# Latent attention: high and low parts of the rotated queries stacked on the array's two halves of rows, two score passes for three

## Chip, cores and metric

One core of a Trainium2 chip runs the whole program. The metric is the device time of one execution in microseconds (us), as the median of several runs. The profile comes from one execution of its own.

## What is computed

The reference is a stack of four transformer-like blocks (windowed attention, latent attention, a recurrent mixer, grouped-query attention). The change touches the second one only. Its core, cut to what matters:

```python
def mla_attend(qn, qp, kn, kp, v):
    scale = (MLA_NOPE + MLA_ROPE) ** -0.5          # 128 and 64
    s = (jnp.einsum('bqhd,bkhd->bhqk', qn, kn)
         + jnp.einsum('bqhr,bkr->bhqk', qp, kp)).astype(jnp.float32) * scale
    p = jax.nn.softmax(s, axis=-1).astype(v.dtype)
    return jnp.einsum('bhqk,bkhd->bqhd', p, v)
```

There are 16 heads, 256 queries and 512 keys (256 context and 256 latent tokens). A score is the sum of a plain part of width 128, with keys of each head, and a rotated part (rope) of width 64, whose key `kp` is one for all heads.

## The kernel before

All products run in the type fp32r, and to keep float32 accuracy every operand is held as two tiles, a high part (the value cast to fp32r) and a low part (the value less its high part). `mm3` (line 349) makes a product of three matmuls, which this text calls passes: high x high, high x low, low x high (lines 352, 353, 354). The product of the two low parts is left out. `hilo` (433) makes the parts: ScalarE casts (436), VectorE subtracts (437).

`mla` (783) works on head groups of two heads (`HG`), eight groups. `project(g + 1)` makes the operands of the next group: it loads weights (`weights`, 327, on the SyncE queue), splits them into `whi` on ScalarE (323) and `wlo` on VectorE (324), multiplies, normalises (`head_norm`, 606) and transposes to feature-major layout (`to_feat`, 640). `project` and the gate's projection are a generator, and `work` (424) takes some steps of it between the attention steps of the current group (`STEPS`), so that TensorE has projections to do while the softmax of a head runs on VectorE and ScalarE. Beside this, `fill` (284) advances a second generator, `mod_steps` (243), which loads tiles of `mod_w` (1 MB each, line 240) into one buffer `mraw` in this stage and multiplies them (line 260).

`head_norm` for rotated queries: a copy of the bank (611), ScalarE's square (613), VectorE's sum (615), a scaling (453), the power -1/2 on GpSimd (456), then four VectorE steps (621, 624, 628, 629) for norm and rotation. Its tiles, `hr`, `sq` and `w`, come from one ring of four scratch tiles (`t512`, 146). The rotated queries of four heads are made at a time: every second head group, for two token tiles of 128 tokens each (lines 868 to 876). A normalised tile isn't transposed at once: it goes into the list `late`, and the oldest entry is transposed when more than `LATE` = 2 are in it. The rotated query tiles are `qph` and `qpl`, with 64 rows in use; the rotated keys are `kph` and `kpl` (`ev_kv`, 814), also with 64 rows, made once for each of four token tiles before the head loop.

The scores of a head and one token tile go into one PSUM bank: three passes over 128 rows of the array for the plain part, three over 64 rows for the rotated part (lines 925, 926). `probs` (552) takes the maximum, the exponential and the scaling; `attend` (575) transposes the probabilities (591) and multiplies with the values.

Which instruction runs when on an engine is decided by the framework's scheduler when the program is built; on the chip each engine keeps that order, and semaphores make it wait for the others. Work of different parts of the text is therefore interleaved on every engine.

Of the kernel before, what the change touches and what calls it, by code (L numbers as in the profile page):

```python
# [10 lines left out]
F32 = mybir.dt.float32  # L11
F32R = mybir.dt.float32r
AF = mybir.ActivationFunctionType
ALU = mybir.AluOpType
# [4 lines left out]
P = 128  # L19
D = 2048  # L20
KD = D // P
NT = 512
NC = 256
L = 64
HG = 2
# [91 lines left out]
class Net:  # L117
# [665 lines left out]
    def mla(self, kvb):  # L783
        nc, I, h = self.nc, self.I, self.h
        scale = 192 ** -0.5
        with self.tc.tile_pool(name="mla", bufs=1) as ph:
# [2 lines left out]
            tk = self.rope_tables(ph, I["pe_cos"], I["pe_sin"], "mk_pe", "mk_pes", 64, "mk")  # L789
            ckh = ph.tile([P, 2, NT], F32R, name="ckh")  # L790
            ckl = ph.tile([P, 2, NT], F32R, name="ckl")
            kph = ph.tile([64, 1, NT], F32R, name="kph")
            kpl = ph.tile([64, 1, NT], F32R, name="kpl")
            cqh = ph.tile([P, 4, NC], F32R, name="cqh")
            cql = ph.tile([P, 4, NC], F32R, name="cql")

            def low(ps, n, nb, dh, dl, s, gain):
                sq = self.t512("sq", cols=n)
                ss = self.small(1, "ss")
                nc.scalar.activation(sq, ps, AF.Square, accum_out=ss)  # L800
                rs = self.small(1, "rs")
                self.rpow(rs, ss, 1.0 / n, EPS)
                q = self.t512("cq", cols=n)
                nc.vector.tensor_scalar(q, ps, rs, None, ALU.mult)
                pb = self.bank("tr")
                for b in range(nb):
                    nc.tensor.transpose(pb[:, b * P : (b + 1) * P], q[:, b * P : (b + 1) * P], self.ident)
                for b in range(nb):
                    self.hilo(dh[:, b, s], dl[:, b, s], pb[:, b * P : (b + 1) * P], self.v(gain, b))
# [4 lines left out]
            def ev_kv(t, ps):  # L814
                s = slice(t * P, (t + 1) * P)
                rope = None if t < 2 else (tk[0][:, t - 2, :], tk[1][:, t - 2, :])
                kp = self.head_norm(ps[:, 256:320], 1, 64, gain=self.row("mk_pe"), rope=rope)
                self.to_feat(kp, 1, 64, kph[:, :, s], kpl[:, :, s])
                low(ps[:, 0:256], 256, 2, ckh, ckl, s, "kva_g")

            def ev_cq(t, ps):
# [2 lines left out]
            for t in range(4):  # L824
                ev_kv(t, kvb[t])
# [3 lines left out]
            qp = {}  # L829

            def two_toks(w, act, kc, toks):

                ws = list(self.weights(w, kc, HG * P))
                for t0 in toks:
                    bank = self.acc()
                    for t in (t0, t0 + 1):
                        s = slice(t * P, (t + 1) * P)
                        out = bank[:, (t - t0) * HG * P : (t - t0 + 1) * HG * P]
                        for k, wh, wl in ws:
                            self.mm3(out, act[0][:, k, s], act[1][:, k, s], wh, wl, k == 0, k == kc - 1)  # L840
                        yield None
                    yield t0, bank

            def project(g, t_):

                new = lambda n, shape: ph.tile(shape, F32R, tag=n, name=self.nm(n), bufs=2)
                kq = {n: new(n, [P, HG, NT]) for n in ("kh", "kl")}
                kq.update({n: new(n, [P, 4, HG * P]) for n in ("vh", "vl")})
                kq.update({n: new(n, [P, HG, NC]) for n in ("qh", "ql")})
                t_.update(kq)  # L850
                late = []

                def norms():

                    for got in two_toks(I["mla_kb"][g], (ckh, ckl), 2, (0, 2)):
                        yield
                        if got:
                            k = self.head_norm(got[1], 2 * HG, P)
                            s = slice(got[0] * P, (got[0] + 2) * P)
                            late.append((k, 2 * HG, P, *(pairs_of(kq[n], s) for n in ("kh", "kl"))))  # L860
                            yield "group"
                    for got in two_toks(I["mla_qb"][g], (cqh, cql), 4, (0,)):
                        yield
                        if got:
                            q = self.head_norm(got[1], 2 * HG, P)
                            late.append((q, 2 * HG, P, *(pairs_of(kq[n], slice(0, NC)) for n in ("qh", "ql")), self.qkg))
                            yield "group"
                    if g4 not in qp:
                        qp[g4] = [ph.tile([64, 4, NC], F32R, tag=n, name=self.nm(n), bufs=2) for n in ("qph", "qpl")]
                        banks = {}  # L870
                        yield from self.mm_tok_steps(banks, I["mla_qp"][g4], (cqh, cql), 4, 256, range(2))
                        for t in range(2):
                            s = slice(t * P, (t + 1) * P)
                            q = self.head_norm(banks[t][:, :256], 4, 64, rope=(tq[0][:, t, :], tq[1][:, t, :]))
                            late.append((q, 4, 64, qp[g4][0][:, :, s], qp[g4][1][:, :, s]))
                            yield "group"
                    for got in two_toks(I["mla_vb"][g], (ckh, ckl), 2, (0, 2)):
                        yield
                        if got:
                            v = got[1].rearrange("p (t d) -> p t d", t=2)  # L880
                            self.hilo(kq["vh"][:, got[0] : got[0] + 2, :], kq["vl"][:, got[0] : got[0] + 2, :], v)
                            yield "group"

                g4 = g * HG // 4
                for what in norms():
                    yield
                    if what and len(late) > LATE:
                        self.to_feat(*late.pop(0))
                        yield
                while late:  # L890
                    self.to_feat(*late.pop(0))
                    yield

            def pairs_of(t, s):
                return t[:, :, s].rearrange("p h (t q) -> p t h q", t=2)

            def jobs(g, nxt, banks):

                gate, owed = self.gate_job(I["mla_g"][g], NC, banks, HG), 0.0
                for _ in project(g + 1, nxt) if g + 1 < 16 // HG else ():  # L900
                    yield
                    owed += GRATE[g % 2]
                    while owed >= 1.0:
                        owed -= 1.0
                        if next(gate, "end") != "end":
                            yield
                yield from gate

            cur = {}
            for _ in project(0, cur):  # L910
                pass
            for g in range(16 // HG):
                oT = ph.tile([P, HG, NC], F32, tag="oT", name=self.nm("oT"), bufs=2)
                oT = [oT[:, hh, :] for hh in range(HG)]
                banks, nxt = [], {}
                self.beside(jobs(g, nxt, banks), STEPS[g % 2] if g < 7 else 16, (1 + 2 * MB + MT) * HG)
                kh, kl, vh, vl, qh, ql = (cur[n] for n in ("kh", "kl", "vh", "vl", "qh", "ql"))
                qph, qpl = qp[g * HG // 4]
                for hh in range(HG):
                    hd = HG * g + hh  # L920
                    prs = []
                    for t in range(2):
                        s = slice(t * P, (t + 1) * P)
                        sc = self.bank("sc")
                        self.mm3(sc, qh[:, hh, s], ql[:, hh, s], kh[:, hh, :], kl[:, hh, :], True, False)
                        self.mm3(sc, qph[:, hd % 4, s], qpl[:, hd % 4, s], kph[:, 0, :], kpl[:, 0, :], False, True)
                        prs.append(self.probs(sc, NT, scale, None, ph, hd))
                    self.work()
                    po = self.bank("pv")
                    self.attend(  # L930
                        prs, NT, lambda c: vh[:, c, hh * P : (hh + 1) * P], lambda c: vl[:, c, hh * P : (hh + 1) * P],
                        po[:, :NC], ph, bool(MB),
                    )
                    nc.scalar.copy(oT[hh], po[:, :NC])
                    if MT:
                        self.work()
                self.work(last=True)
                self.gate_out(oT, HG * g, banks, NC, self.oscr, ph)
                cur = nxt
# [1060 lines left out]
```

## Time and profile before

| | |
|---|---|
| median of 3 runs | 3359.38 us (3355.93 to 3361.99) |
| profiled execution | 3360.43 us, its span 3358.6 us |
| TensorE (PE) busy | 3206.8 us, 95% |
| VectorE (DVE) busy | 2050.3 us, 61% |
| ScalarE (ACT) busy | 1543.9 us, 46% |
| granted TensorE clock, mean | 0.984 of full speed |

The span is what the profiler recorded from the first to the last instruction; the execution's time has some 1.8 us more around it. A share of busy time is a mean over stages with different limits, so a change in one stage is judged from that stage's own window. Matmuls are pipelined: the next one starts before the one before it has ended, so the cost of a pass is the distance from its start to the next start. PE is the matmuls, PEld the loading of the stationary operand, which can run beside a matmul. A form such as 64\*128 is the part of the array in use, rows by columns.

### The profile page before, as it was taken

Reading aid. Unit: us, or ns where it says so; the run is one execution under the profiler, and the core shown is the slowest. Engines: PE = TensorE matmul, PEld = TensorE weight load, DVE = VectorE, ACT = ScalarE, POOL = GpSimd, SP = SyncE. Lnnn points to the kernel's source line nnn. Section 1 sums busy time; section 2 is a strip of 40 time slices with the busy share of each in tenths; the row PEclk is TensorE's granted clock in tenths of the full one; section 3 lists DMA queues with packets and bytes.
Section 4 is the critical chain, followed back from the end, with each engine's and each line's share of the span. In section 5 each row is a group of like instructions: output and inputs, shape, how many; then the busy total and the mean of one; then the engine's idle time right before and its main releaser. Section 6 shows DMA issues by size and latency. Waiting matters only on the chain.

```text
span 3358.6 us, 56061 instructions
## 1 busy us (share of the span) xinstructions
PE 3206.8 (95%) x21218; PEld 2374.5 (71%) x21218; DVE 2050.3 (61%) x4487; ACT 1543.9 (46%) x3461; POOL 195.4 (6%) x277
## 2 busy tenths in 40 slices
PE   5999999999999999999999999999999999899997
PEld 2567777767777777886666666566666668678887
DVE  2446455543476665557766777577677536857766
ACT  2424444442366565643444444343444423646654
POOL 0000000000001010000000000000000001200000
PEclk8999999989999999999999999999999999999999
DMA  7843434357654655765333333334334464534354
GB/s 302 307 163 127 145 138 145 131 191 288 224 164 147 212 197 204 278 228 173 119 117 117 117 114 106 105 96 150 115 107 135 173 237 139 182 126 138 136 175 155
DMA packets 270784, 556.27 MB, mean 166 GB/s; under 512 B 122928, under 2 KB 150704, under 8 KB 244912
## 3 DMA queue, kind: packets, MB, share of 16 engines
q1 hardware_dynamic: 270512, 552.68, 48.5%
q8 instruction: 167, 2.74, 0.3%
q14 instruction: 105, 0.86, 0.1%
HBM read 517.46 MB, written 35.13 MB: 165 GB/s over the span
## 4 chain that ended last, share of the span: by engine, by line
PE 80%; DVE 8%; DMA 4%; ACT 3%; issue 2%; POOL 2%; SPq 0%; POOLq 0%; DVEq 0%; ACTq 0%
PE a L352 19%; PE a L354 17%; PE a L353 17%; PE mv L260 6%; PE gram L1241 2%; DMA mraw<-mod_w 2%; POOL rs L456 2%; PE ptr L591 1%; PE sc L352 1%; DVE wlo L324 1%; PE chain L1376 1%; PE chain L1380 1%; PE inv L1341 1%; PE chain L1388 1%; ACT whi L323 1%
## 5 line engine op out<-in xcount | busy, mean ns | idle before, releaser
L324 DVE TENSOR_TENSOR wlo<-raw,whi 128x512 fp32r<-128x512 f32 (+2 forms) x1000 | 659.8, 667 | 592.1 <-ACT whi L323 556.2
L352 PE MATMUL a<-hhi,whi 128*128 128x512 f32 (+1 forms) x2752 | 976.8, 356 | 15.4 <-ACT whi L323 11.0
L323 ACT CAST whi<-raw 128x512 fp32r<-128x512 f32 (+2 forms) x1000 | 593.3, 599 | 826.4 <-PE a L353 471.6
L354 PE MATMUL a<-hhi,wlo 128*128 128x512 f32 (+1 forms) x2752 | 947.5, 348 | 5.9 <-DVE wlo L324 5.5
L353 PE MATMUL a<-hlo,whi 128*128 128x512 f32 (+1 forms) x2752 | 952.1, 346 | 0.1
L352 PEld LDWEIGHTS a<-hhi,whi 128*128 128x128 f32 x2752 | 522.9, 190 | 160.3 <-issue 52.8
L354 PEld LDWEIGHTS a<-hhi,wlo 128*128 128x128 f32 x2752 | 520.8, 190 | 70.6 <-DVE wlo L324 11.4
L353 PEld LDWEIGHTS a<-hlo,whi 128*128 128x128 f32 x2752 | 523.8, 190 | 55.1 <-issue 4.1
L352 PE MATMUL a<-whi,hhi 128*128 128x512 f32 (+1 forms) x672 | 261.9, 400 | 18.5 <-ACT sq L613 5.9
L260 PE MATMUL mv<-mraw,cs 128*32 128x512 f32 x1536 | 251.0, 634 | 19.5 <-DMA mraw<-mod_w 19.2
L353 PE MATMUL a<-wlo,hhi 128*128 128x512 f32 (+1 forms) x672 | 263.8, 393 | 0.3
L456 POOL TENSOR_TENSOR rs<-st,mhalf 128x4 f32<-128x4 f32 (+3 forms) x109 | 140.4, 1288 | 2102.2 <-DVE st L453 1952.0
L354 PE MATMUL a<-whi,hlo 128*128 128x512 f32 (+1 forms) x672 | 259.7, 389 | 0.1
L352 PEld LDWEIGHTS a<-whi,hhi 128*128 128x128 f32 x672 | 126.6, 190 | 76.3 <-issue 22.2
L353 PEld LDWEIGHTS a<-wlo,hhi 128*128 128x128 f32 x672 | 128.6, 191 | 30.1 <-DVE wlo L324 4.6
L354 PEld LDWEIGHTS a<-whi,hlo 128*128 128x128 f32 x672 | 128.4, 191 | 26.4 <-issue 1.1
L565 ACT ACTIVATE pr<-sc,nm 128x512 f32<-128x512 f32 (+1 forms) x128 | 81.1, 633 | 93.1 <-DVE nm L562 66.7
L1385 ACT ACTIVATE SD<-SV,DL 64x64 f32<-64x64 f32 x224 | 77.2, 345 | 80.4 <-DVE SV L1399 77.2
L1399 DVE SCALAR_TENSOR_TENSOR SV<-chain,DL,SD 64x64 f32<-64x64 f32 x224 | 63.3, 283 | 71.2 <-PE chain L1393 62.9
L556 DVE TENSOR_REDUCE mx<-sc 128x1 f32<-128x512 f32 (+1 forms) x128 | 79.0, 617 | 41.6 <-PE sc L354 24.7
L260 PEld LDWEIGHTS mv<-mraw,cs 128*32 128x32 f32 x1536 | 36.1, 110 | 93.0 <-issue 52.2
L572 ACT ACTIVATE pr<-pr,rc 128x512 f32<-128x512 f32 (+1 forms) x128 | 85.6, 669 | 22.0 <-DVE rc L571 21.9
(371 smaller groups left out, 4460.3 us busy)
## 6 DMA issues: line engine op xcount, KB each, us to landing
mraw<-mod_w SPq DMA_DIRECT2D x192, 1024.0 KB, 4.9
raw<-od_in SPq DMA_DIRECT2D x88, 512.0 KB, 3.3
raw<-swa_in SPq DMA_DIRECT2D x72, 512.0 KB, 3.3
raw<-ev_rkv SPq DMA_DIRECT2D x64, 384.0 KB, 3.5
raw<-ev_in SPq DMA_DIRECT2D x48, 512.0 KB, 3.7
raw<-swa_out SPq DMA_DIRECT2D x40, 512.0 KB, 5.6
raw<-ev_out SPq DMA_DIRECT2D x40, 512.0 KB, 3.4
raw<-mla_g SPq DMA_DIRECT2D x64, 256.0 KB, 3.0
```

Source lines behind the costliest of these rows:

```text
L260: nc.tensor.matmul(pb[32 * j : 32 * j + 32, :], cs[:, 32 * k + 30 - 2 * n : 32 * k + 62 - 2 * n], raw[:, j, :], start=(n == 0 and q == 0), ...
L323: nc.scalar.copy(whi, raw)
L324: nc.vector.tensor_tensor(wlo, raw, whi.bitcast(F32), op=ALU.subtract)
L352: mm(out, ah, bh, start=first, stop=False, skip_group_check=shared)
L353: mm(out, ah, bl, start=False, stop=False, skip_group_check=shared)
L354: mm(out, al, bh, start=False, stop=last, skip_group_check=shared)
L456: self.nc.gpsimd.tensor_tensor(dst, stv, mv, op=ALU.pow)
L556: nc.vector.reduce_max(mx, sc, axis=AX.X)
L565: nc.scalar.activation(pr[:, :n], sc, AF.Exp, scale=scale, bias=nm, accum_out=sm)
L572: nc.scalar.activation(pr[:, :n], pr[:, :n], AF.Copy, scale=rc)
L1241: mm(pb[:, (c - c4) * P : (c - c4 + 1) * P], lhs, AQ[r_, hh, c, :], start=True, stop=True)
L1385: nc.scalar.activation(SD[r_], SV[r_, hh, c, :], AF.Copy, scale=DL[r_, c : c + 1])
```

## The change

The rotated queries get one tile `qp` of 128 rows: rows 0 to 63 hold the high part, rows 64 to 127 the low part of the same 64 features. The rotated keys are stored twice, in both halves of `kph` (high parts) and of `kpl` (low parts). One pass with `kph` then gives high x high plus low x high, one with `kpl` high x low plus low x low: two passes over 128 rows in place of three over 64 rows. (The product of the low parts, left out before, is now included.)

To bring the same values into both halves, `twice` copies a normalised token-major tile on ScalarE so that each head's 64 columns stand there two times (128 columns); the transposes then give 128 rows. `stack` replaces `to_feat` for the queries: four transposes, a cast of all 128 rows, and on VectorE, for rows 64 to 127 alone, the subtraction of the just cast values in place. For the keys, `to_feat` is called with 128 rows instead of 64. Entries of `late` for the rotated queries have two members, by which `feat` tells them from the others.

```diff
--- before.py
+++ after.py
@@ -789,8 +789,29 @@
             tk = self.rope_tables(ph, I["pe_cos"], I["pe_sin"], "mk_pe", "mk_pes", 64, "mk")
             ckh = ph.tile([P, 2, NT], F32R, name="ckh")
             ckl = ph.tile([P, 2, NT], F32R, name="ckl")
-            kph = ph.tile([64, 1, NT], F32R, name="kph")
-            kpl = ph.tile([64, 1, NT], F32R, name="kpl")
+
+
+            kph = ph.tile([P, 1, NT], F32R, name="kph")
+            kpl = ph.tile([P, 1, NT], F32R, name="kpl")
+
+            def twice(q, nh):
+
+                t = self.t512("tw", cols=nh * P)
+                nc.scalar.copy(
+                    t.rearrange("p (h a d) -> p h a d", h=nh, a=2),
+                    q.rearrange("p (h d) -> p h d", h=nh).unsqueeze(2).broadcast_to([P, nh, 2, 64]),
+                )
+                return t
+
+            def stack(q, dst):
+
+                pb = self.bank("tr")
+                for n in range(4):
+                    nc.tensor.transpose(pb[:, n * P : (n + 1) * P], q[:, n * P : (n + 1) * P], self.ident)
+                pv = pb.rearrange("p (h t) -> p h t", h=4)
+                nc.scalar.copy(dst, pv)
+                lo = slice(64, P)
+                nc.vector.tensor_tensor(dst[lo], pv[lo], dst[lo].bitcast(F32), op=ALU.subtract)
             cqh = ph.tile([P, 4, NC], F32R, name="cqh")
             cql = ph.tile([P, 4, NC], F32R, name="cql")
 
@@ -815,7 +836,7 @@
                 s = slice(t * P, (t + 1) * P)
                 rope = None if t < 2 else (tk[0][:, t - 2, :], tk[1][:, t - 2, :])
                 kp = self.head_norm(ps[:, 256:320], 1, 64, gain=self.row("mk_pe"), rope=rope)
-                self.to_feat(kp, 1, 64, kph[:, :, s], kpl[:, :, s])
+                self.to_feat(twice(kp, 1), 1, P, kph[:, :, s], kpl[:, :, s])
                 low(ps[:, 0:256], 256, 2, ckh, ckl, s, "kva_g")
 
             def ev_cq(t, ps):
@@ -866,13 +887,13 @@
                             late.append((q, 2 * HG, P, *(pairs_of(kq[n], slice(0, NC)) for n in ("qh", "ql")), self.qkg))
                             yield "group"
                     if g4 not in qp:
-                        qp[g4] = [ph.tile([64, 4, NC], F32R, tag=n, name=self.nm(n), bufs=2) for n in ("qph", "qpl")]
+                        qp[g4] = ph.tile([P, 4, NC], F32R, tag="qp", name=self.nm("qp"), bufs=2)
                         banks = {}
                         yield from self.mm_tok_steps(banks, I["mla_qp"][g4], (cqh, cql), 4, 256, range(2))
                         for t in range(2):
                             s = slice(t * P, (t + 1) * P)
                             q = self.head_norm(banks[t][:, :256], 4, 64, rope=(tq[0][:, t, :], tq[1][:, t, :]))
-                            late.append((q, 4, 64, qp[g4][0][:, :, s], qp[g4][1][:, :, s]))
+                            late.append((twice(q, 4), qp[g4][:, :, s]))
                             yield "group"
                     for got in two_toks(I["mla_vb"][g], (ckh, ckl), 2, (0, 2)):
                         yield
@@ -882,13 +903,18 @@
                             yield "group"
 
                 g4 = g * HG // 4
+
+                def feat():
+                    args = late.pop(0)
+                    (stack if len(args) == 2 else self.to_feat)(*args)
+
                 for what in norms():
                     yield
                     if what and len(late) > LATE:
-                        self.to_feat(*late.pop(0))
+                        feat()
                         yield
                 while late:
-                    self.to_feat(*late.pop(0))
+                    feat()
                     yield
 
             def pairs_of(t, s):
@@ -915,7 +941,7 @@
                 banks, nxt = [], {}
                 self.beside(jobs(g, nxt, banks), STEPS[g % 2] if g < 7 else 16, (1 + 2 * MB + MT) * HG)
                 kh, kl, vh, vl, qh, ql = (cur[n] for n in ("kh", "kl", "vh", "vl", "qh", "ql"))
-                qph, qpl = qp[g * HG // 4]
+                qpe = qp[g * HG // 4]
                 for hh in range(HG):
                     hd = HG * g + hh
                     prs = []
@@ -923,7 +949,8 @@
                         s = slice(t * P, (t + 1) * P)
                         sc = self.bank("sc")
                         self.mm3(sc, qh[:, hh, s], ql[:, hh, s], kh[:, hh, :], kl[:, hh, :], True, False)
-                        self.mm3(sc, qph[:, hd % 4, s], qpl[:, hd % 4, s], kph[:, 0, :], kpl[:, 0, :], False, True)
+                        for n, kp in enumerate((kph, kpl)):
+                            nc.tensor.matmul(sc, qpe[:, hd % 4, s], kp[:, 0, :], start=False, stop=n == 1)
                         prs.append(self.probs(sc, NT, scale, None, ph, hd))
                     self.work()
                     po = self.bank("pv")
```

## Rows read from the trace of the kernel before

**Rows 1.** The page: busy us of each engine (share) xinstructions.
```profile
PE 3206.8 (95%) x21218; PEld 2374.5 (71%) x21218; DVE 2050.3 (61%) x4487; ACT 1543.9 (46%) x3461; POOL 195.4 (6%) x277
```

**Rows 2.** Windows, head loop: length; PE, PEld, DVE, ACT, POOL busy; clock, DMA.
```profile
1036.60:1343.40 306.80, 299.15 (x2123) 237.21 (x2120) 187.72 (x403) 182.64 (x396) 29.30 (x27) 0.99 0.57 198
```

**Rows 3.** Waits of PE's matmuls, the same stretch: total us, times, longest.
```profile
PE a L354 <- DVE wlo L324: 2.8, 3, 1.2
PE a L352 <- ACT whi L323: 2.1, 3, 1.1
PE a L353 <- DVE wlo L324: 1.2, 3, 0.4
```

**Rows 4.** Timeline of PE, two scores of one head: start us, us, instruction.
```profile
1203.19 0.28 PE L354 MATMUL a<-hhi,wlo 128*128 128x256 f32 x1
1203.31 0.39 PE L352 MATMUL sc<-kh,qh 128*128 128x512 f32 x1
1203.54 0.40 PE L353 MATMUL sc<-kl,qh 128*128 128x512 f32 x1
1203.77 0.40 PE L354 MATMUL sc<-kh,ql 128*128 128x512 f32 x1
1204.10 0.50 PE L352 MATMUL sc<-kph,qph 64*128 64x512 f32 x1
1204.44 0.39 PE L353 MATMUL sc<-kpl,qph 64*128 64x512 f32 x1
1204.67 0.38 PE L354 MATMUL sc<-kph,qpl 64*128 64x512 f32 x1
1204.99 0.50 PE L352 MATMUL sc<-kh,qh 128*128 128x512 f32 x1
...
1206.76 0.38 PE L353 MATMUL a<-wlo,ckh 128*128 128x256 f32 x1
1206.99 0.28 PE L354 MATMUL a<-whi,ckl 128*128 128x256 f32 x1
```

**Rows 5.** Tile kh, 32 first passes: idle before its instructions, us, times.
```profile
  issue: 5.0, 14
```

**Rows 6.** Tile kph: one of the three rotated passes; duration ns min/median/max.
```profile
L354 PE MATMUL sc<-kph,qpl x32: 383/393/393, 1038.9 to 1343.0; 64*128 64x512 f32 x32
```

**Rows 7.** Tile qph: its cast and the subtraction after it.
```profile
L436 ACT CAST qph<-tr x8: 579/581/583, 1031.1 to 1287.6; 64x512 fp32r<-64x512 f32 x8
L437 DVE TENSOR_TENSOR qpl<-tr,qph x8: 671/674/683, 1032.6 to 1288.3; 64x512 fp32r<-64x512 f32 x8
```

**Rows 8.** Tile tr, 960:1360 us: the cast of a full-height tile.
```profile
L436 ACT CAST kh<-tr x16: 563/584/591, 1020.6 to 1326.4; 128x512 fp32r<-128x512 f32 x16
```

**Rows 9.** Line L480: a copy with each value repeated 64 times, on ACT.
```profile
L480 ACT COPY rse<-rs x16: 602/608/618, 1532.8 to 2528.8; 128x512 f32<-128x512 f32 x16
```

**Rows 10.** Timeline, the first score of the head loop.
```profile
1037.08 0.58 ACT L436 CAST qph<-tr 64x512 fp32r<-64x512 f32 x1 [0.99 <-PE tr L644]
1037.70 0.68 DVE L437 TENSOR_TENSOR qpl<-tr,qph 64x512 fp32r<-64x512 f32 x1 [0.44 <-ACT qph L436]
1038.26 0.60 PE L352 MATMUL sc<-kph,qph 64*128 64x512 f32 x1
```

**Rows 11.** Timeline, normalisation of one rotated query tile: square to last rotation step.
```profile
1104.63 0.38 ACT L613 ACTIVATE sq<-a 128x256 f32<-128x256 f32 x1
1105.90 1.30 POOL L456 TENSOR_TENSOR rs<-st,mhalf 128x4 f32<-128x4 f32 x1 [11.31 <-DVE st L453]
...
1109.30 0.41 DVE L629 TENSOR_TENSOR hr<-hr,w 128x256 f32<-128x256 f32 x1
```

**Rows 12.** Waits of ACT, the head loop.
```profile
ACT hr L637 <- POOL rs L456: 30.3, 19, 3.7
```

**Rows 13.** Tile mraw, the head loop: 32 loads, their time to landing, waits.
```profile
L240 SPq DMA_DIRECT2D mraw<-mod_w x32: 327/328/984, 1053.9 to 1325.1; - x32
DMA to landing us min/median/max: 4.6/4.8/6.8
```

## The prediction

> **What bounds the kernel now.** I read the page first, then the stretch that the change touches, then the passes themselves. On the page TensorE is busy for 95% of the span, VectorE for 61%, ScalarE for 46% [rows 1]. Such a share mixes stages, so the windows view of the latent attention's head loop comes next, from its first score (1036.6 us) to its last (1343.4 us): 306.80 us long, PE busy for 299.15 of them, DVE for 187.72, ACT for 182.64, clock 0.99 [rows 2]. PE's idle time is 306.80 - 299.15 = 7.65 us, and the waits list gives its three largest causes, all for weights that ACT and DVE convert: 2.8 + 2.1 + 1.2 = 6.1 us [rows 3]. So PE sets the pace of this stretch, and a pass taken off PE should come off the time, unless what PE rarely waits for today comes late.
>
> What a pass costs is read from starts, not durations, because passes overlap. Back-to-back 128-row passes with 512 columns start 0.23 us apart (1203.31, 1203.54, 1203.77), those with 256 columns 0.12 apart (1203.19, 1203.31). Two 64-row passes with 512 columns also start 0.23 apart (1204.44, 1204.67): half the rows gain nothing. But each change of height costs extra: 1203.77 to 1204.10 is 0.33, 1204.10 to 1204.44 is 0.34, back to 128 rows 1204.67 to 1204.99 is 0.32, and after the second score a 256-column pass takes 1206.76 to 1206.99, 0.23 for 0.12 [rows 4]. So a change of height costs 0.10 before the first pass of the new height and 0.11 at it, 0.2 us in all. That it is the height and not the new accumulation is seen at tile kh: of 32 first passes of a score, 14 show an unexplained idle time ahead of them, 5.0 us in all, 0.36 each [rows 5]. The loop has 16 heads with two scores each, and the program text puts these two next to each other, so some 16 first passes follow a 64-row group and some 16 a 128-row pass; the one at 1203.31 is of the second sort and starts at the ordinary pitch.
>
> **Passes removed.** One head's two scores run from 1203.31 to 1206.76, and 0.11 of the pass after them is still theirs: 3.45 + 0.11 = 3.56 us for 12 passes. Afterwards they are ten 128-row passes: 10 x 0.23 = 2.30 us. That is 1.26 us for a head. A rotated pass occurs 32 times [rows 6], so there are 16 such pairs: 16 x 1.26 = 20.2 us off PE. Of these 32 x 0.23 = 7.4 us is the third pass, and 12.8 us is 64 changes of height at 0.2.
>
> A sentence of the Trainium skill speaks against counting this in full: "Perfetto Trace Analysis", section Identifying the Most-Contended Engine, says that matmul busy time is a poor measure of a loaded TensorE and that weight loading's busy share is a good one. Here that share is 237.21 of 306.80, 77% [rows 2]; read so, 77% of the saving, 15.6 us, would show. The starts leave no free slot between passes [rows 4], so the trace speaks for the whole; no term below hangs on this.
>
> **Transposes, cast, subtraction.** Their number stays. The query cast grows from 64 to 128 rows: 581 ns [rows 7] against 584 for a full-height cast [rows 8], 0. The subtraction keeps its 64 x 512 (674 ns [rows 7]), but writes rows 64 to 127: 0. DVE and POOL get no new instruction. No DMA is added or moved, so no queue's order changes by design. The query tiles shrink to one where there were two; nothing uses the space.
>
> **Copies added.** `twice` puts each value into both halves, on ACT. The nearest row is a copy that spreads values over 128x512: 608 ns [rows 9]. Eight query tiles cost 8 x 0.61 = 4.9 us, two of them ahead of the loop; the four key tiles are a quarter of the width, so between 0.15 and 0.61 each. In the loop ACT goes from 182.6 to 186.3 us of some 287, hidden as long as PE's converted weights are ready. Bounds for what PE feels: below, 0; above, a doubling of PE's waits on ACT and DVE, 6.1 us [rows 3]. I take 2, nearer to 0: ACT and DVE are idle a third of the loop, but the loop is 7% shorter. The copy's target is from the ring of four scratch tiles; it is asked for when the tile w is done with, which the copy waits for anyway: 0.
>
> **Start of the loop.** The first score waits for its query tile. Before, the first rotated pass (1038.26) needs only the cast (1037.08 + 0.58), and the low part comes from DVE by 1038.38 [rows 10]. Afterwards the first rotated pass needs the low part as well, and the copy of 0.61 stands ahead of the transposes. Between 0 (the three other passes of the score cover it) and 0.61 + 0.68 + the keys' 4 x 0.61 = 3.7 us; I take 1.5, a copy and a subtraction with a little cover. Later query tiles are made one head group ahead.
>
> **Sum.** Profiled execution 3360.43 (span 3358.6 and 1.8 around it) - 20.2 + 2 + 1.5 = 3343.7. The median of the runs, 3359.38, is 1.05 below the profiled one: 3342.7, forecast 3343. Its own range: with no cost at all 3359.4 - 20.2 = 3339.2, with both upper bounds 3359.4 - 20.2 + 6.1 + 3.7 = 3349.0; runs of before differ by 3 either way, and a changed loop shifts the whole order that the scheduler makes: 3336 to 3352.
>
> **Rivals.** *The switch stays.* If the 0.2 us belongs to the change from one operand group to another and not to the height, only the pass goes: 7.4 - 3.5 = 3.9 us, 3355. For it: the rotated passes are never seen at full height. Against: the pass at 1203.31 changes operands at the ordinary pitch [rows 4]. Chance 0.07.
>
> *Given back.* The mod_w tiles go through one buffer in this stage: 32 loads in 306.8 us, one each 9.6 us, landing takes 4.8 (at most 6.8) [rows 13]. A loop shorter by 20 us leaves 9.0 for each, still over 6.8 and the eight passes that free the buffer; only where two steps lie close would PE wait longer. With converted weights late as well, at most the whole 20.2 is given back: 3354 to 3359. Chance 0.08.
>
> *ACT's queue stands behind the copy (slower).* The copy can't run before the last rotation step. One query tile's square starts at 1104.63, POOL's power takes 1105.90 to 1107.20, the last step ends at 1109.71: 1109.71 - 1105.01 = 4.7 us from the square's end [rows 11]. If ACT's order has the copy right behind the square, the weight casts queued behind it wait that long, and PE waits for them and for DVE's subtractions from them. Six copies in the loop x 4.7 = 28 us against 20.2 saved and 1.5 lost at the start: 3359.4 - 20.2 + 1.5 + 28 = 3369. It decides from (20.2 - 1.5) / 6 = 3.1 us of PE stall for each copy. For it: ACT already stands 30.3 us in the loop for POOL's power, in 19 waits of up to 3.7 [rows 12]. Against: all of those leave PE 2.1 us of waits for ACT [rows 3], and between the square and the last step much other work runs on both engines, so the order isn't that of the program text. In a sentence of its own: the Trainium skill, "TensorE: Matmul & The Clock Gate", section Architectural detail, calls ACT's queue a strict FIFO, by which such a copy would block what is behind it; the 30.3 us agree. Chance 0.07.
>
> That the change doesn't do what it says is hardly possible: the passes are written out one by one.
>
> **Chances.** Forecast 0.78, the others 0.07, 0.08, 0.07. A measurement tells 0.2% (6.7 us) from no change: faster 0.78, same 0.15, slower 0.07. The range takes the forecast's, the first rival and half of the second: 3336 to 3357.
>
> **What would show it.** In the trace after: score passes at 0.23 us from first to last, no 0.36 us of weight-load idle before them, `twice` at some 0.6 us, PE busy in the head loop some 20 us less. Wrong would be: 0.33 us between the nope and the rotated passes (the switch stays); PE waits on whi and wlo of over 12 us, or mraw waits of several us (given back); ACT idle of 4 us before each copy with PE idle beside it (slower).

## The result, and the profile after

| | before | after |
|---|---|---|
| median of the runs | 3360.31 us | 3344.61 us |
| ratio after/before, 95% interval | | 0.9949 (0.9932 to 0.9966) |
| profiled execution, its span | 3358.6 us | 3342.8 us |
| head loop, first to last start of a score pass | 306.3 us | 286.8 us |
| from the end of the key/value projection to the first score | 65.5 us | 69.1 us |
| from the last score pass to the end | 2015.6 us | 2015.7 us |

The changed kernel was measured a second time, beside other kernels (label c_after): median 3342.22 us, ratio 0.9949 (0.9935 to 0.9963). So the change makes the kernel 0.5% faster, 17 us with an interval of some 6 either way, and the profiled executions differ by 15.8 us. One of the changed kernel's five executions in the table took 16649.97 us; it is in that median, but not in the ratio (the median of the other four is 3341.43 us).

The page of the changed kernel, span and busy time, stands against [rows 1]:

```profile
span 3342.8 us, 56008 instructions
PE 3188.5 (95%) x21186; PEld 2374.6 (71%) x21186; DVE 2050.8 (61%) x4487; ACT 1547.4 (46%) x3473; POOL 195.3 (6%) x277
```

PE is busy for 18.3 us less (3206.8 to 3188.5), the other engines as long as before, within 4 us. The windows view of the head loop, columns as in [rows 2], from the first score to the last:

```profile
1040.30:1327.40 287.10, 279.53 (x2081) 234.64 (x2079) 186.23 (x402) 182.53 (x401) 29.24 (x27) 0.99 0.61 209
```

The stretch is 287.10 us long where it was 306.80, 19.7 less, and PE's busy time in it falls by 19.6 us (299.15 to 279.53). ACT and DVE do the same work in the shorter time. The clock is 0.99 as before.

Where it went is seen in the timeline of PE, two scores of one head, the lines that answer to [rows 4]:

```profile
1197.21 0.40 PE L352 MATMUL sc<-kh,qh 128*128 128x512 f32 x1
1197.44 0.40 PE L353 MATMUL sc<-kl,qh 128*128 128x512 f32 x1
1197.68 0.39 PE L354 MATMUL sc<-kh,ql 128*128 128x512 f32 x1
1197.91 0.40 PE L953 MATMUL sc<-kph,qp 128*128 128x512 f32 x1
1198.15 0.40 PE L953 MATMUL sc<-kpl,qp 128*128 128x512 f32 x1
1198.38 0.40 PE L352 MATMUL sc<-kh,qh 128*128 128x512 f32 x1
...
1199.30 0.39 PE L953 MATMUL sc<-kpl,qp 128*128 128x512 f32 x1
1199.53 0.28 PE L352 MATMUL a<-whi,ckh 128*128 128x256 f32 x1
```

Ten passes start 0.23 us apart from the first (1197.21) to the pass that follows (1199.53): 2.32 us, where twelve took 3.56. The gaps of 0.32 to 0.34 us are gone, and all forms are 128\*128.

PE's waits in the loop, the list that answers to [rows 3] (total us, times, longest):

```profile
PE ptr L591 <- ACT pr L572: 2.5, 4, 1.6
PE tr L810 <- ACT tw L800: 1.5, 1, 1.5
PE a L352 <- ACT whi L323: 1.2, 2, 1.0
...
PE mv L260 <- DMA mraw<-mod_w: 0.5, 2, 0.3
```

PE now waits less for converted weights (1.2 us for `whi`; `wlo` isn't in the list any more), and instead 2.5 us for probabilities and once 1.5 us for a query copy. PE's idle time in the loop is 287.10 - 279.53 = 7.57 us, where it was 7.65: what is late has changed, but not how much.

One thing got worse, ahead of the loop. From the end of the key/value projection to the first score it takes 69.1 us where it took 65.5. Timeline before (of ACT only; L800 is there the square of the latent key part, at 972.18 right behind a weight cast):

```profile
971.65 0.62 ACT L323 CAST whi<-raw 128x512 fp32r<-128x512 f32 x1
972.18 0.38 ACT L800 ACTIVATE sq<-a 128x256 f32<-128x256 f32 x1
```

The same place after the change. L800 is now the copy `tw`, L821 is that square:

```profile
971.63 0.62 ACT L323 CAST whi<-raw 128x512 fp32r<-128x512 f32 x1
...
975.16 0.28 DVE L633 SCALAR_TENSOR_TENSOR hr<-hr,rs,row_mk_pe 128x64 f32<-128x64 f32 x1 [2.19 <-DMA row_mk_pe<-rows]
975.48 0.30 ACT L800 COPY tw<-hr 128x128 f32<-128x128 f32 x1 [3.24 <-DVE hr L633]
975.69 0.38 ACT L821 ACTIVATE sq<-a 128x256 f32<-128x256 f32 x1
975.83 0.18 PEld L644 LDWEIGHTS tr<-ident,tw 128*128 128x128 f32 x1 [4.56 <-ACT tw L800]
```

ACT reaches the copy of the first key tile at 972.2 and stands 3.24 us, since the keys' norm on DVE waits for a row of gains from memory until 975.16. The square of the latent part needs none of that, but stands behind the copy in ACT's order: 975.69 for 972.18. The latent part is what the first group's keys are made from.

How much of this PE felt is in its windows view, from the last pass of the key/value projection to the first cast of `kh`, and from there to the first score (length; PE busy, xinstructions; granted clock; DMA share, GB/s). The first two lines are of before, the last two of after:

```profile
971.25:1020.56 49.31, 41.12 (x201) 0.90 0.54 181
1020.56:1036.70 16.14, 12.66 (x96) 0.95 0.20 55
971.23:1022.73 51.50, 40.60 (x201) 0.93 0.51 173
1022.73:1040.30 17.57, 13.80 (x109) 1.00 0.25 76
```

In the first part PE has the same 201 instructions and idles 51.50 - 40.60 = 10.90 us where it idled 8.19. In the second its idle time is nearly the same (3.77 for 3.48), but 13 more instructions run there, passes of 256 columns of other projections: 1.5 us at 0.12 each. They aren't extra work: the scheduler put them ahead of the first score, and the loop has them no longer. So some 1.5 of the 3.6 us is work moved out of the loop, and nearly as much of the loop's saving is its other side.

### The profile page after: what moved, and what is told of

The parts are those of the page before. It is cut to its first block, busy times and chain, and to the rows that moved or that the text cites. A ratio compares the mean times of both kernels' runs of the same rounds, so it can differ in the third digit from the quotient of the medians.

```text
span 3342.8 us, 56008 instructions
## 1 busy us (share of the span) xinstructions
PE 3188.5 (95%) x21186; PEld 2374.6 (71%) x21186; DVE 2050.8 (61%) x4487; ACT 1547.4 (46%) x3473; POOL 195.3 (6%) x277
## 4 chain that ended last, share of the span: by engine, by line
PE 80%; DVE 9%; ACT 4%; DMA 3%; issue 2%; POOL 2%; SPq 0%; POOLq 0%; DVEq 0%; ACTq 0%
PE a L352 19%; PE a L354 18%; PE a L353 17%; PE mv L260 6%; PE gram L1268 2%; POOL rs L456 2%; DMA mraw<-mod_w 2%; PE ptr L591 1%; DVE wlo L324 1%; PE chain L1407 1%; PE chain L1403 1%; PE inv L1368 1%; PE chain L1415 1%; PE chain L1431 1%; ACT whi L323 1%
## 5 line engine op out<-in xcount | busy, mean ns | idle before, releaser
L1417 ACT COPY SV<-chain 64x64 f32<-64x64 f32 x128 | 26.5, 207 | 150.1 <-DVE SV L1416 145.9
```

## The experiments

The head loop's length and the two parts of the start are read from starts of instructions in each kernel's own trace: the last pass of the key/value projection, the first cast of `kh` for head group 0 (the latent part has then passed its norm, its transposes and a projection), the first score pass, the last score pass. In brackets stand what PE idled in the first part, PE's instructions in the second, and the granted clock of each part. Each ratio is against executions of the kernel before that were taken along with that kernel's.

| kernel | median us | ratio to before | projection to first kh cast, us (idle; clock) | kh cast to first score, us (instructions; clock) | head loop, us (clock) |
|---|---|---|---|---|---|
| before | 3360.31 | 1 | 49.3 (8.2; 0.90) | 16.1 (96; 0.95) | 306.3 (0.99) |
| after | 3344.61 | 0.9949 (0.9932 to 0.9966) | 51.5 (10.9; 0.93) | 17.6 (109; 1.00) | 286.8 (0.99) |
| c_after | 3342.22 | 0.9949 (0.9935 to 0.9963) | 51.4 (10.8; 0.93) | 17.6 (108; 1.00) | 284.1 (1.00) |
| e1_third_full | 3349.92 | 0.9975 (0.9964 to 0.9987) | 51.6 (9.8; 0.90) | 17.6 (109; 1.00) | 290.8 (1.00) |
| e7_two_zero | 3356.64 | 0.9991 (0.9982 to 1.0) | 52.0 (11.2; 0.93) | 17.6 (108; 1.00) | 298.7 (1.00) |
| e2_two_short | 3352.30 | 0.9973 (0.9962 to 0.9984) | 49.0 (7.8; 0.90) | 16.0 (96; 0.96) | 299.1 (1.00) |
| e3_low_first | 3336.15 | 0.9926 (0.9912 to 0.9939) | 46.1 (7.5; 0.96) | 20.3 (134; 1.00) | 284.7 (0.99) |
| e4_fused | 3339.04 | 0.9938 (0.9926 to 0.9951) | 48.2 (6.8; 0.89) | 17.0 (97; 0.96) | 284.1 (1.00) |
| e5_fused_low | 3339.63 | 0.9933 (0.992 to 0.9946) | 46.7 (7.3; 1.00) | 16.3 (97; 1.00) | 285.6 (1.00) |
| e6_copy_again | 3341.93 | 0.9948 (0.9934 to 0.9962) | 51.6 (9.9; 0.90) | 18.2 (113; 1.00) | 286.4 (1.00) |
| e8_before_low | 3358.63 | 0.9992 (0.9982 to 1.0003) | 47.8 (7.2; 0.96) | 16.1 (95; 0.95) | 305.7 (0.99) |
| e9_keys_fused | 3338.69 | 0.9931 (0.9915 to 0.9948) | 49.0 (7.4; 0.90) | 17.6 (108; 1.00) | 284.2 (1.00) |

Two theories stood against each other on the saving: that a change of the array's height costs 0.2 us and a pass 0.23 (12.8 and 7.4 us in all), or that only passes count or the height plays no part. Two stood on the start: that ACT's queue stands behind the copies, or that the scheduler's order or the first score's need for the low part makes it late.

**The spread first, c_after.** The changed kernel again, the order of every engine the same.

> The changed kernel once more, unchanged, for the spread: with the same order of instructions the head loop should be 286.8 us again within 1 us, first score at 1040.3, time 3338 to 3347. Were the loop to differ by 3 us, differences of that size between the other kernels would say nothing.

The first parts agree to 0.2 us, the loop was 284.1, 2.7 shorter, and the time behind the loop 2008.2 instead of 2015.7 us. The expectation of 1 us was wrong, and the two traces show where the difference lies. PE in the windows view, of the loop and of one stretch in it, each time first the earlier execution, then c_after:

```profile
1040.30:1327.07 286.77, 279.20 (x2079) 0.99 0.61 210
1041.12:1325.21 284.09, 276.22 (x2078) 1.00 0.61 212
1049.00:1055.80 6.80, 6.45 (x29) 0.50 0.12 17
1049.80:1056.60 6.80, 6.45 (x44) 1.00 0.35 123
```

In the earlier execution the granted clock stood at the lower of its two levels (0.50, 1.2 instead of 2.4 GHz) for these 6.8 us, and PE got 29 instructions done where c_after did 44. Half of 6.8 us is 3.4, an estimate of the loss; the loops differ by 2.7. Shortly before, PE had waited 1.61 us for probabilities, but in c_after it had too, so why the clock fell in one alone stays open. Over the whole execution the granted clock is 0.985 and 0.988; 0.003 of 3340 us is 10 us, and the spans differ by 9.4. So single executions can be compared only beside their clocks. The loop of before also has two stretches at 0.50, 5.2 us together: at most 2.6 us, by the same estimate.

**Pass or height, e2_two_short and e1_third_full.** The first is the kernel before with the third of the short passes left out:

```diff
-self.mm3(sc, qph[:, hd % 4, s], qpl[:, hd % 4, s], kph[:, 0, :], kpl[:, 0, :], False, True)
+for n, kp in enumerate((kph, kpl)):
+    nc.tensor.matmul(sc, qph[:, hd % 4, s], kp[:, 0, :], start=False, stop=n == 1)
```

> The kernel before with two 64-row passes instead of three; the product of the queries' low parts with the keys' high parts is left out of the score. Theory (a change of height costs 0.2 us, a pass 0.23): the gaps of 0.32 to 0.34 us around the rotated passes stay, the head loop goes from 306.8 to 299.4 us, the time to 3353. Rival (the saving of the change is that of the pass and what follows from it): the loop goes to 287 us and the time to 3344 or, without the copies, 3341.

The loop was 299.1 us where 299.4 was expected, the time by the ratio 9.1 us below before (0.9973). Its timeline of PE keeps the gaps around the short passes, 0.33 going in and 0.32 coming out:

```profile
1200.25 0.40 PE L353 MATMUL sc<-kl,qh 128*128 128x512 f32 x1
1200.48 0.40 PE L354 MATMUL sc<-kh,ql 128*128 128x512 f32 x1
1200.81 0.50 PE L927 MATMUL sc<-kph,qph 64*128 64x512 f32 x1
1201.15 0.40 PE L927 MATMUL sc<-kpl,qph 64*128 64x512 f32 x1
1201.47 0.50 PE L352 MATMUL sc<-kh,qh 128*128 128x512 f32 x1
```

The second is the changed kernel with a third pass at full height, against zeros:

```diff
-for n, kp in enumerate((kph, kpl)):
-    nc.tensor.matmul(sc, qpe[:, hd % 4, s], kp[:, 0, :], start=False, stop=n == 1)
+for n, kp in enumerate((kph, kpl, kpz)):
+    nc.tensor.matmul(sc, qpe[:, hd % 4, s], kp[:, 0, :], start=False, stop=n == 2)
```

> The changed kernel with a third full-height pass for each score, against a tile of zeros, so six passes of 128 rows instead of six of two heights; the result is the same. Theory (a change of array height costs 0.2 us, a pass 0.23): every pass of a score starts 0.23 us after the one before, the head loop grows by 32 x 0.23 = 7.4 us, from 287 to 294.5, and the time is 3352 us. Rival (only the number of passes counts): the loop is back at 307 us and the time at 3361.

Here six passes run at one height, 0.23 us apart, though the stationary and the moving operand change at the fourth:

```profile
1197.98 0.48 PE L352 MATMUL sc<-kh,qh 128*128 128x512 f32 x1
...
1198.53 0.40 PE L354 MATMUL sc<-kh,ql 128*128 128x512 f32 x1
1198.77 0.40 PE L957 MATMUL sc<-kph,qp 128*128 128x512 f32 x1
1199.00 0.39 PE L957 MATMUL sc<-kpl,qp 128*128 128x512 f32 x1
1199.23 0.40 PE L957 MATMUL sc<-kpz,qp 128*128 128x512 f32 x1
1199.47 0.39 PE L352 MATMUL sc<-kh,qh 128*128 128x512 f32 x1
```

The loop was 290.8 us, not 294.5, but 15.5 below that of before with the same number of passes, so the rival falls: most of the saving is the height. The four kernels make a square. Beside c_after, at the same clock, the third pass at full height is worth 290.8 - 284.1 = 6.7 us; at half height it is 306.3 - 299.1 = 7.2, of which 1 to 2 us is the lower clock in before's loop. Predicted were 7.4. The height is worth 306.3 - 290.8 = 15.5 us at three passes and 299.1 - 284.1 = 15.0 at two; predicted were 12.8. In both differences some 1.5 us is the 13 moved passes, and 1 to 3 us is clock, so 11 to 13 us remain by estimate. By the ratios the third pass costs the changed kernel 0.9975 - 0.9949 = 0.0026, 8.7 us, give or take some 6.

**Is PE still the bound after the change, e7_two_zero.** One more pass against zeros, `(kph, kpl, kpz, kpz)`.

> The changed kernel with two more full-height passes against zeros for each score (the result is the same), seven in all. Theory (TensorE sets the loop's pace also after the change): 64 passes of 0.23 us add 14.8 us to the changed kernel's loop, 301.5 us, time 3359. Rival (after the change other waits share the bound, and added passes fill idle time): the first extra pass added 4.0 us instead of 7.4, the second adds more than the first, and the loop is at 296 to 299 us.

The tile of zeros, 64 passes at the same duration as the others:

```profile
L957 PE MATMUL sc<-kpz,qp x64: 389/396/401, 1041.2 to 1338.7; 128*128 128x512 f32 x64
```

The loop was 298.7 us, in the interval that I had given to the rival. But the base was wrong: it was a loop with the clock at the lower level for 6.8 us. Beside c_after, at the same clock, the 64 passes added 298.7 - 284.1 = 14.6 of 14.8 us, and by the ratios 0.0042, 14.1 us. So PE sets the pace after the change too, and the added passes filled no idle time worth mentioning: the theory holds.

**Without copies on ACT, e4_fused.** The last step of `head_norm` writes both halves itself: for the rotated tiles the add of line 629 reads both operands twice over, for the two context key tiles the scaling of line 633.

```diff
...
+tv = two.rearrange("p (h a d) -> p h a d", h=nh, a=2)
+dup = lambda t: hv(t).unsqueeze(2).broadcast_to([P, nh, 2, hd])
+nc.vector.tensor_tensor(tv, dup(raw), dup(w), op=ALU.add)
...
-self.to_feat(twice(kp, 1), 1, P, kph[:, :, s], kpl[:, :, s])
+self.to_feat(kp, 1, P, kph[:, :, s], kpl[:, :, s])
...
-late.append((twice(q, 4), qp[g4][:, :, s]))
+late.append((q, qp[g4][:, :, s]))
```

The doubled tile is then no longer from the ring of four scratch tiles but has two buffers of its own, so e4, e5 and e9 differ from the changed kernel in that as well.

> The changed kernel without copies on ACT: the last step of the norm on VectorE writes its result into both halves (0.69 instead of 0.41 us for a query tile by a 128x512 add). Theory (the copies cost the start of the loop 3.7 us and nothing inside it): the first score starts at 1036.6 to 1037.5 instead of 1040.3 us, the head loop stays at 287 within 1 us, the time is 3341. Rival (the start is late because the first score needs the low part too): the first score moves by under 1 us, the time stays at 3344.

The start fell from 69.1 to 65.2 us, that of before: PE idles 6.8 us in its first part where it idled 10.9, and the second has 97 instructions where it had 109. The square of the latent part (here L827) is back right behind a weight cast:

```profile
971.24 0.62 ACT L323 CAST whi<-raw 128x512 fp32r<-128x512 f32 x1
971.76 0.38 ACT L827 ACTIVATE sq<-a 128x256 f32<-128x256 f32 x1
```

and the doubling add takes 0.68 us on DVE for a query tile:

```profile
L632 DVE TENSOR_TENSOR tw<-hr,w x10: 281/681/691, 982.8 to 1266.3; 128x512 f32<-128x512 f32 x8, 128x128 f32<-128x128 f32 x2
```

The loop was 284.1 us, as in c_after, with ten more instructions in it (2088 for 2078) and 1.9 us at the lower clock. So the copies cost the start, as the theory had it. In the loop this execution leaves them some 2 us by estimate (ten passes at 0.12, and 0.9 for the clock), that of e5 below nothing (285.6 us with 12 more instructions), so "nothing inside the loop" isn't shown closer than that.

**Keys or queries, e9_keys_fused.** As e4_fused, but the query copies stay on ACT.

> The changed kernel with the keys' halves written by VectorE and the query copies still on ACT. Theory (the start's 3.6 us are 2.1 from the key copies and 1.5 from the query copies): from the end of the projection to the first kh cast 48.2 to 49.4 us instead of 51.5, from there to the first score 17.6 as in the changed kernel, loop 284 to 287, time 3341. Rival (the query copies carry the delay): the first part stays at 51.5 us and the time at 3343.

49.0 and 17.6 us, as expected: the key copies account for 2.5 us up to the first `kh` cast, by PE's idle time for 3.5 (10.9 to 7.4). The 1.5 us behind it go with the query copies, but they are the moved passes: 108 instructions here, 109 in after, 97 in e4, 96 in before, while PE's idle time there is 3.5 to 3.9 us in all four. That part is moved, not lost.

**More of the suspected cost, e6_copy_again.** Each query copy is followed by a copy of the tile onto itself, `nc.scalar.copy(t, t)`.

> The changed kernel with every query copy on ACT followed by a second one of the same size in place (8 more of 0.62 us), so the suspected cost is doubled. Theory (ACT has room in the loop, the copies cost only at its start): the loop stays at 287 within 2 us, the first score comes 0.6 to 1 us later, time 3345 to 3346. Rival (ACT's queue stands behind the copies and PE with it): the loop grows by 6 x 0.62 = 3.7 us or more, time 3349 or later.

Groups by line of ACT in the loop (x count, busy us, mean ns, idle before):

```profile
L800 ACT COPY tw<-hr 128x512 f32<-128x512 f32 x6 | 3.7, 621 | 6.4 <-DVE hr L629 6.4
L805 ACT COPY tw<-tw 128x512 f32<-128x512 f32 x6 | 3.7, 619 | 0.0
```

With 3.7 us more work on ACT in the loop, it took 286.4 us, and the ratio is 0.9948. The theory had said 287 within 2; but beside c_after, at the same clock, the loop is 2.3 us longer, between the theory and the rival's 3.7. Whether a part of the second copies reaches PE isn't settled by this run. The part between `kh` cast and first score grew from 17.6 to 18.2 us, with 113 instructions in place of 109: again passes ahead of the first score.

**The order of the text, e3_low_first and e8_before_low.** In `ev_kv` the latent part (`low`) is put ahead of the rotated keys, in the changed kernel and in the kernel before.

```diff
+low(ps[:, 0:256], 256, 2, ckh, ckl, s, "kva_g")
 kp = self.head_norm(ps[:, 256:320], 1, 64, gain=self.row("mk_pe"), rope=rope)
 self.to_feat(...)
-low(ps[:, 0:256], 256, 2, ckh, ckl, s, "kva_g")
```

> The changed kernel, with the latent key part of each token tile put ahead of the rotated keys in the program text. Theory (ahead of the head loop ACT stands behind the keys' copies, and the square of the latent part is queued behind them): that square runs before the copy, the first cast of kh comes back from 1022.7 to about 1020.6 us, the first score starts about 2 us earlier than 1040.3, time 3342.5. Rival (the later start is the scheduler's other order or the extra work, not the queue): the first score stays at 1040 and the time at 3344.6.

> The kernel before, with only the latent key part of each token tile put ahead of the rotated keys in the program text. From the end of the key and value projection to the first cast of kh it took 49.4 us before the change, 51.5 after it, 46.1 with the same reordering after it. If that reordering gained by taking ACT from behind the copies, there is little to gain here where there are no copies: 49 us, first score at 65.5 us after the projection, time 3360. If the reordering is worth 3 us by itself, it is 46 us here as well and the time is 3357.

The two parts of the start in e3:

```profile
973.26:1019.36 46.10, 38.57 (x179) 0.96 0.55 183
1019.36:1039.62 20.26, 17.49 (x134) 1.00 0.28 91
```

In the changed kernel the first part fell by 5.4 us, to 46.1, more than the copies had cost. But 22 of its 201 instructions, passes of 256 columns of a query projection, run behind the first `kh` cast instead: 2.6 us at 0.12, and the reason why the first score came only 2.8 us earlier (66.4 for 69.1). What was cured is PE's idle time: 10.9 to 7.5 us. In the kernel before the same edit gained 1.5 us (49.3 to 47.8), between the two expectations, 1.0 of it in idle time (8.2 to 7.2), the rest at a higher clock (0.96 for 0.90). So the order is worth some 1 us by itself, and the other 2.4 are what the latent part loses behind the copies, if the two simply add.

**Both, e5_fused_low.**

> No copies on ACT (VectorE writes both halves) and the latent key part ahead of the rotated keys. Theory (both cured the same thing, ACT standing behind the keys' copies): no more than either alone, the first score at 1036 us, the head loop at 284 to 287, the time at 3338. Rival (two separate costs): the first score at 1033 or earlier and the time at 3334.

The first score came 63.1 us after the projection, 2.1 earlier than in e4_fused, which looks as if the two edits added up in part. Their first parts, e4 and then e5, show that they don't:

```profile
970.84:1019.01 48.17, 41.39 (x201) 0.89 0.55 184
971.62:1018.35 46.73, 39.41 (x201) 1.00 0.56 189
```

The instructions are the same in number, PE's idle time is 6.8 and 7.3 us, and the difference is busy time: the clock was 0.89 in e4 and 1.00 in e5. In the second parts it was 0.96 and 1.00, with 97 instructions and 3.9 us of idle time in both. So the theory holds: both edits cure the same wait.

The medians of e3, e4, e5 and e9 lie at 3336 to 3340 us, and their intervals overlap with each other and touch that of the changed kernel. All four beat both kernels by the medians; that they beat the changed kernel isn't shown by the intervals, and which of the four is best was not told apart.

## Why the prediction was right, step by step

**Passes removed.** The forecast took 20.2 us off PE; the loop shrank by 19.5 us at a like clock (the 22.2 of c_after has a clock of 1.00 against 0.99). Some 1.3 to 1.5 us of that is the passes that now run ahead of the first score, and the lower clock cost the loop after the change 3.4 us by estimate, that of before 2.6. So 18 to 19 us remain for the change itself, 1 or 2 below the forecast. Two scores of a head, 3.56 us before and 2.32 after, times 16 are 19.8. The split of the sum, 12.8 for the height and 7.4 for the pass, is borne out by e1 and e2 to within some 1.5 us.

**The height costs, not the operands.** The argument from one pass at an ordinary pitch [rows 4] and from 14 of 32 idle times [rows 5] was right: at full height the rotated passes follow at 0.23 us. In the loop of before, all 16 first passes behind a 64-row pass start 0.31 to 0.32 us after it; after the change all 16 behind a rotated pass start 0.23 us after it. The first rival (the switch stays) falls by the trace after.

**PE's waits in the loop.** Taken as 2 us more; PE's idle time didn't grow (7.57 us for 7.65). The second rival, given back, falls with it: PE's matmuls waited 0.5 us for mod_w tiles.

**The start.** This is the term that was mis-sized: 1.5 us taken, 3.6 measured (69.1 - 65.5), at the upper end of 3.7 that was given. Of the 3.6 us PE idled 3.0 more, and 1.5 are moved passes, less what a higher clock gave back. The reason given for the term was also wrong in part. The cast and subtraction of [rows 10] are those of the second token tile, the first having been cast from 1031.1 on [rows 7]. After the change the first score didn't wait for that tile's low part: its first rotated pass started at 1041.07, the subtraction at 1041.37. The passes of a score wait for their own token tile only. What cost most were the key copies: I had priced their durations, 4 times 0.15 to 0.61, but not what stands behind them on ACT, though the prediction names just that mechanism for the loop. The 3.24 us themselves are a row of gains that lands late, before as well as after the change; whether loading it earlier would do as much as taking the copy off ACT was not run. The key copy's own duration is 0.3 us; the waits of ACT at the copies carry the cost (the 4.2 us for L633 are at the two context key tiles):

```profile
L800 ACT COPY tw<-hr x12: 297/618/627, 975.5 to 1273.8; 128x512 f32<-128x512 f32 x8, 128x128 f32<-128x128 f32 x4
...
  DVE hr L629: 10.8, 9
  DVE hr L633: 4.2, 2
```

**ACT's queue behind the copies, the slower rival.** The mechanism exists and decides the idle time of the start, but not the loop: there the list of ACT's waits has five ahead of copies, 6.9 us in all, and PE waited for a copy once, 1.5 us. The reason given against it held: the scheduler puts the copy near the time at which its input is ready, and other work lies between. The Trainium skill, "TensorE: Matmul & The Clock Gate", section Architectural detail, calls ACT's queue a strict FIFO; the 3.24 us ahead of the first key copy, with the square behind it, agree.

**Cast and subtraction.** 586 ns for 581, and 694 for 674 on rows 64 to 127, as good as nothing:

```profile
L812 ACT CAST qp<-tr x8: 578/586/596, 1033.7 to 1276.3; 128x512 fp32r<-128x512 f32 x8
L814 DVE TENSOR_TENSOR qp<-tr,qp x8: 686/694/695, 1034.3 to 1277.4; 64x512 fp32r<-64x512 f32 x8
```

**The sum.** 0.0 up to the projection's end, +3.6 at the start, -19.5 in the loop, +0.1 behind it: -15.8, the difference of the spans. The forecast had +1.5, -20.2, +2: -16.7. So the total was met because two misses of 2 us, at the start and in PE's waits, stood on opposite sides. In part that is luck; in part, the 1.5 us of moved passes, it is one and the same time, added at the start and taken from the loop, which cancels in the total.

The Trainium skill's page "Perfetto Trace Analysis", section Identifying the Most-Contended Engine, gives the weight-load share, beside the floating-point rate reached, as a measure of how close TensorE is to its limit. That a saving shows in proportion to this share, 77% (15.6 us), was my own reading of it. It isn't borne out in the loop, where 19.5 us appeared at a like clock, 18 to 19 of them from the change; the share rose to 234.64 of 287.10, 82%.

## What to carry to other kernels

Read the price of a matmul from the distance between starts, and look at the passes on either side: half of the array's rows saved no time at all, while each change of height between groups of passes cost 0.2 us, so short contractions are better filled up (here with the low part of the operand) than left short. A small copy added on an in-order engine is to be priced by what stands behind it while it waits for its input, not by its duration; it cost most ahead of the loop, where PE idled for it. If the step before can write its result twice, the copy and ACT's wait at it go away together. Where a scheduler makes the order, count the instructions on both sides of a mark before calling a longer stretch a loss: 13 passes ahead of the first score were only moved.

## What the runs showed that I had not expected

The same program with the same order on every engine took 286.8 and 284.1 us for the head loop and 2015.7 and 2008.2 us for what follows it, and most of that goes with the granted clock: 6.8 us at its lower level in the one loop, none in the other. Beside the first execution instead of c_after, e1's third pass would seem to cost 4.0 us and e7's two 11.9, and e5 would seem to gain 2.1 us over e4. A change of 0.2% is told by medians of several runs; a single execution is read beside its clock and its count of instructions.
